# First layer's down-projection: sixth product ahead of the fifth, three norms set apart, two loads put under holds

## The chip, the cores and the metric

One core of a Trainium2 chip runs the whole program. The metric is the device time of one execution in microseconds (us). The reported time is the median of several runs.

## The reference, cut to what matters

The program is one inference step of a two-layer encoder on 1024 prompt rows and 8 x 16 sample rows, 1152 rows of 1024 columns, all float32. Each layer has a mixer and then a GEGLU channel mixer with a causal convolution, and each is closed by a layer norm. The part at hand is the end of layer 0's channel mixer: the down-projection and the norm behind it.

```python
ALPHA = (2 * DEPTH) ** 0.25                       # DEPTH = 2
...
out = (gelu(g) * a) @ w_down                      # (1152, 2816) @ (2816, 1024)
...
x = layer_norm(ALPHA * x + (1 + g_f) * f, ln_g[l, 1], ln_b[l, 1])
```

## The kernel before

The 1152 rows are nine tiles of 128. `down1` (L1466) multiplies the activations, 22 row blocks of 128 (`NFF`), kept transposed in DRAM as `actD`, by `wdn`. Tiles 0 to 5 go through a scheme of seven products in place of eight (Winograd's form of Strassen's): the inner dimension is paired, block 2m with 2m + 1 (`NK` = 11 steps), the rows are halved into tiles 0 to 2 and 3 to 5, and the columns into two halves of 512. Its operands are slices of `actD` and `wdn`, sums of them that earlier code has put in `actS` and `wT`, and for product 5 a difference of two halves of `wdn` that is made on the spot: two loads (L1536, L1537) and a subtraction on POOL (L1538).

A float32 product is three matmuls of rounded parts. For each operand SP loads it (L1498 weights, L1505 activations), ACT casts it to the high part (L184), and DVE subtracts to get the low part (L195). One step m of a product is nine matmuls (L1511): three tiles by three parts, 512 columns each, into three of the eight PSUM banks. With `keep` the last steps are gathered, so that each bank is finished, and read out by `done(i)`, before the next.

The order of the products before is 1 (banks A = 0, 1, 2), 2 (C = 5, 6, 7), 5 (B = 3, 4, 5), 6 (on top of 1 in A), 3 (on top of 5 in B), 7 (on top of 6 in A), 4 (B). The read-outs are `to_c11` (ACT copies C, DVE adds A: L1592, L1593), `to_p5`, `to_u2`, `to_c12` (L1603), `to_c22` (L1607, and ACT's copy L1608) and `to_c21`. `gate` multiplies by the gate (L1559), and `head` adds the residual (L1574), loaded by `fetch_row`.

`norm` calls `norm_tail`: statistics on DVE (L998 to L1002), a square root on ACT (L987) with its refinement on DVE (L988 to L992), a scaling on DVE (L1037), eight transposes on PE in two groups of four (L1047) into two banks, their read-out by DVE (L1055) and ACT (L1059, L1063), and writes to DRAM (L1066, L1068, L1072). Tiles 0 to 2 are normed while product 7 runs, at its steps 2, 5 and 8.

Tiles 8, 6 and 7 then go through a plain product, `block`, over 22 row blocks. Its weights come through `wload` (the load is L199), the first two in `ahead`, just before product 4's last steps. Tiles 3 to 5 are gated and normed inside its first steps.

The order of the instructions on each engine is set by a planner (a scheduler with a timeline model), which takes the code's order as a priority and moves instructions within their dependences. `with self.tc.issue_after(ins)` adds order edges from `ins` to instructions of the block. SP issues all loads and writes here, and at most eight are outstanding: each waits for the one eight before it.

Of the kernel before, what the change touches and what calls it, by code (L numbers as in the profile page):

```python
# [106 lines left out]
class Trunk:  # L107
# [1359 lines left out]
    def down1(self, xsrc, xdst, affs, act_sums):  # L1467
# [52 lines left out]
        def fetch(q, m):  # L1520
            e, o = 2 * m, 2 * m + 1
# [13 lines left out]
            r, b = diffs.next(), diffs.next()  # L1535
            nc.sync.dma_start(r, wdn[e][:, lo_half])  # L1536
            nc.sync.dma_start(b, wdn[e][:, hi_half])  # L1537
            nc.gpsimd.tensor_sub(r, b, r)  # L1538
            w = subs.next()
# [3 lines left out]
        def product(q, banks, new=True, keep=0, hook=None, ahead=lambda: None, done=lambda i: None):  # L1543
            for m in range(NK - keep):
                a, w = fetch(q, m)
                for i in range(3):
                    mm(self.bank(banks[i]), a, i, w, new and m == 0, m == NK - 1)
                if hook:
                    hook(m)
# [26 lines left out]

        A, B, C = (0, 1, 2), (3, 4, 5), (5, 6, 7)

# [23 lines left out]
        def to_c12(i):  # L1602
            nc.vector.tensor_add(u2[i], self.bank(B[i]), u2[i])  # L1603
            gate(u2[i], u2[i], i, 1)
# [6 lines left out]
        def to_c21(i):  # L1611
            nc.vector.tensor_sub(u3[i], u3[i], self.bank(B[i]))

        product(1, A, hook=start)
        aff = affs()
        product(2, C, keep=2, done=to_c11)
        product(5, B, done=to_p5)
        product(6, A, new=False, hook=norm_rows, done=to_u2)
        for t in range(3):
            fetch_row(t)  # L1620
        product(3, B, new=False, done=to_c12)

        hf1, rows = Ring([self.hf]), []

        def done(m):
            if m in (0, 3, 6):
                rows.append(head(m // 3))
            if m in (2, 5, 8):
                with self.tc.issue_after(self.downmm):
                    norm(m // 3, rows[m // 3], hf1, C[1:3])  # L1630

# [3 lines left out]
        def more(m):  # L1635
            if m in (1, 3, 6):
                fetch_row(3 + (1, 3, 6).index(m))

# [10 lines left out]
        def ahead():  # L1649
            nonlocal acts  # L1650
            self.ws, acts = Ring(plain), Ring(highs)
            firsts.extend(load(j) for j in range(2))

# [5 lines left out]
        keep = KEEP[0]  # L1659
        product(4, B, keep=keep, hook=more, ahead=ahead, done=to_c21)  # L1660
        rows = []
        for j in range(NFF - keep):
# [3 lines left out]
            if j == 0:  # L1666
                for i in range(3):
                    gate(u3[i], u3[i], 3 + i, 0)
                    rows.append(head(3 + i))
                self.take_w0(F32R)  # L1670
# [532 lines left out]
```

## Time and profile before

| what | us |
|---|---|
| median of 3 runs | 2722.82 |
| lowest, highest | 2721.62, 2728.88 |
| profiled execution | 2716.27 |
| its span | 2714.5 |
| PE busy | 2606.1 (96%) |
| DVE busy | 1980.8 (73%) |
| ACT busy | 1365.4 (50%) |
| POOL busy | 1028.1 (38%) |

PE is TensorE's matmuls, DVE VectorE, ACT ScalarE, POOL GpSimd, and SP the engine that issues transfers (SPq is its queue). A row of a timeline gives start, duration, engine, line, operation, output<-input and a count, and in brackets the engine's idle time ahead of it with what ended it. A stretch's PEclk is the granted clock of TensorE as a share of 2.4 GHz. "DMA share" is the mean busy share of the core's 16 DMA engines.

### The profile page before, as it was taken

What the parts mean: (1) busy time and instruction counts of PE and PEld (TensorE: products, weight loads), DVE (VectorE), ACT (ScalarE), POOL (GpSimd) and SP (SyncE); (2) the same over time, 40 slices, a digit from 0 to 9 for tenths busy, and PEclk for the clock granted to TensorE, in tenths of its full rate; (3) what the DMA queues carried; (4) which work ended last, traced back from release to release, by engine and by line L of the source; (5) the groups of instructions that cost most, each with busy time, mean ns of one, the idle gap of its engine ahead of it and who ended that gap; (6) DMA issues with size and microseconds to landing.
All of it is one profiled execution on the core that took longest, in us unless ns stands there. A gap on an engine that the chain in (4) does not pass through costs nothing.

```text
span 2714.5 us, 47659 instructions
## 1 busy us (share of the span) xinstructions
PE 2606.1 (96%) x17295; PEld 2326.4 (86%) x17295; DVE 1980.8 (73%) x3997; ACT 1365.4 (50%) x2855; POOL 1028.1 (38%) x792
## 2 busy tenths in 40 slices
PE   7999889999999999999999999989999999999997
PEld 6997768989999997878898888867899999998886
DVE  4476777787777687787854677777788877778668
ACT  3475734433343345654446666672445454556553
POOL 3032623367666644011220121252367666552101
PEclk9999999999999999999999999999999999999999
DMA  9656534566656548866758556783544334349673
GB/s 326 211 153 204 156 121 168 184 243 229 227 183 206 188 156 298 298 218 219 255 196 263 144 153 187 218 243 123 183 153 163 140 126 150 119 146 315 208 233 124
DMA packets 251564, 531.49 MB, mean 196 GB/s; under 512 B 39904, under 2 KB 108464, under 8 KB 251328
## 3 DMA queue, kind: packets, MB, share of 16 engines
q1 hardware_dynamic: 251328, 528.44, 59.3%
q8 instruction: 136, 2.23, 0.3%
q14 instruction: 100, 0.82, 0.1%
HBM read 396.17 MB, written 141.61 MB: 198 GB/s over the span
## 4 chain that ended last, share of the span: by engine, by line
PE 67%; DVE 12%; DMA 10%; ACT 4%; issue 4%; POOL 3%; SPq 1%; DVEq 0%; POOLq 0%; ACTq 0%
PE PS L1241 23%; PE PS L1511 9%; PE PS L327 8%; PE PS L314 8%; PE PS L1750 5%; PE PS L610 3%; PE PS L588 2%; DVE F L1290 2%; DVE wl L195 2%; PE PS L559 1%; PE PS L241 1%; PE PS L562 1%; PE PS L301 1%; DMA ws<-in_adaw_dram 1%; PE PS L737 1%
## 5 line engine op out<-in xcount | busy, mean ns | idle before, releaser
L1241 PE MATMUL PS<-H,wh 128*128 128x320 f32 (+1 forms) x2624 | 401.8, 294 | 0.0
L1241 PEld LDWEIGHTS PS<-H,wh 128*128 128x128 f32 x2624 | 364.5, 189 | 0.4 <-issue 0.4
L195 DVE TENSOR_TENSOR wl<-F,wh 128x512 fp32r<-128x512 f32 (+3 forms) x245 | 244.3, 1005 | 69.7 <-ACT wh L184 64.9
L1201 DVE TENSOR_TENSOR F<-PS,F 128x256 f32<-128x256 f32 (+1 forms) x446 | 196.1, 451 | 111.9 <-PE PS L1241 103.7
L184 ACT CAST wh<-F 128x512 fp32r<-128x512 f32 (+3 forms) x245 | 144.8, 602 | 248.0 <-PE PS L1241 125.9
L1241 PE MATMUL PS<-H,wl 128*128 128x256 f32 (+1 forms) x1312 | 230.5, 297 | 8.2 <-DVE wl L195 4.3
L1241 PEld LDWEIGHTS PS<-H,wl 128*128 128x128 f32 x1312 | 192.4, 189 | 17.0 <-issue 4.8
L1241 PE MATMUL PS<-xa,wh 128*128 128x320 f32 (+1 forms) x1328 | 204.3, 295 | 0.0
L1241 PEld LDWEIGHTS PS<-xa,wh 128*128 128x128 f32 x1328 | 185.7, 190 | 0.0
L648 POOL TENSOR_TENSOR F<-F,x2r 64x512 f32<-64x512 f32 x62 | 79.2, 1278 | 204.0 <-DVE F L624 170.6
L184 ACT CAST wh<-ws 128x512 fp32r<-128x512 f32 (+1 forms) x140 | 100.0, 717 | 110.3 <-DMA ws<-in_wup_dram 43.7
L1290 DVE SCALAR_TENSOR_TENSOR F<-F 128x1024 f32<-128x1024 f32 (+2 forms) x160 | 141.3, 929 | 7.9 <-ACT F L1329 7.5
L1361 POOL TENSOR_TENSOR F<-F 128x1152 f32<-128x1152 f32 x43 | 122.9, 2858 | 53.3 <-DVE F L1354 22.8
L184 ACT CAST H<-H 128x384 fp32r<-128x384 f32 (+3 forms) x158 | 94.4, 610 | 92.4 <-DMA H<-actD 52.8
L195 DVE TENSOR_TENSOR H<-H 128x384 fp32r<-128x384 f32 (+2 forms) x144 | 101.5, 720 | 51.6 <-ACT H L184 51.5
L195 DVE TENSOR_TENSOR wl<-ws,wh 128x512 fp32r<-128x512 f32 (+1 forms) x122 | 120.2, 987 | 25.8 <-ACT wh L184 21.7
L314 PE MATMUL PS<-H,w0r 128*128 128x384 f32 (+1 forms) x720 | 137.2, 340 | 0.3 <-ACT H L184 0.3
L327 PE MATMUL PS<-xa,H 128*128 128x512 f32 x504 | 128.4, 395 | 5.0 <-ACT xa L184 3.3
L526 DVE CUSTOM_DVE_ANT_0 F<-PS,F,C 128x256 f32<-128x256 f32 (+3 forms) x208 | 97.3, 480 | 49.2 <-PE PS L562 25.3
L314 PE MATMUL PS<-H,wh 128*128 128x384 f32 (+1 forms) x672 | 132.6, 339 | 0.0
L314 PEld LDWEIGHTS PS<-H,w0r 128*128 128x128 f32 x720 | 124.5, 188 | 2.3 <-ACT H L184 0.6
L1241 PE MATMUL PS<-xa,wl 128*128 128x256 f32 (+1 forms) x664 | 120.1, 302 | 4.6 <-DVE F L1201 2.8
(374 smaller groups left out, 6700.5 us busy)
## 6 DMA issues: line engine op xcount, KB each, us to landing
ws<-in_adaw_dram SPq DMA_DIRECT2D x63, 512.0 KB
ws<-in_wup_dram SPq DMA_DIRECT2D x51, 512.0 KB
F<-in_adaw_dram SPq DMA_DIRECT2D x49, 512.0 KB
w0f<-in_wdn_dram SPq DMA_DIRECT2D x44, 512.0 KB
F<-in_wup_dram SPq DMA_DIRECT2D x37, 512.0 KB
xa<-kH SPq DMA_DIRECT2D x60, 256.0 KB
F<-in_wdn_dram SPq DMA_DIRECT2D x60, 256.0 KB
xd<-F SPq DMA_DIRECT2D x27, 512.0 KB
```

Of the source, the lines that this page charges most:

```text
L184: nc.scalar.copy(out, in_)
L195: self.eng(el).tensor_sub(lo, src, hi.bitcast(F32))
L314: mm = self.nc.tensor.matmul(out[:, 0:n], w[a][:, k * 128 : k * 128 + 128], H[:, p, k, s0 : s0 + n], start=i == 0, stop=i == 23)
L327: self.nc.tensor.matmul(out[:, 0:n], H[:, p, j * kn + k, t0 : t0 + 128], w[a][:, k * n : k * n + n], start=i == 0, stop=i == 23,)
L526: nc.vector.tensor_tensor_reduce(out=p[:, c0 : c0 + w], in0=ps, in1=b, scale=1.0, scalar=init, op0=ALU.add, op1=ALU.min, accum_out=nm)
L610: mm = nc.tensor.matmul(ob[:, i0 * 128 : (i0 + n) * 128], vst[a][:, kt, :], pp[:, m * 128 : (m + n) * 128], start=cnt == 0, stop=cnt == to ...
L1201: nc.vector.tensor_add(d, v(ps), a if len(a.shape) == 3 else v(a))
L1241: self.pairmm = nc.tensor.matmul(ps[:, 0:m], w[a][:, k * 128 : k * 128 + 128], x(p, k, n), start=start and c == 0, stop=c == 11, skip_grou ...
L1290: nc.vector.scalar_tensor_tensor(o, u, cw[:, cc, i : i + 1], o, op0=ALU.mult, op1=ALU.add)
L1361: (nc.vector if l == 0 and j == NFF - 1 else nc.gpsimd).tensor_mul(yg, yg, ya)
L1511: self.downmm = nc.tensor.matmul(ps, a[p][:, i * 128 : i * 128 + 128], w[q], start=first and c == 0, stop=last and c == 2, skip_group_chec ...
L1750: self.downmm = nc.tensor.matmul(ps, a[p][:, i * 128 : i * 128 + 128], w[q], start=first and c == 0, stop=last and c == 2, skip_group_chec ...
```

## The change

Five things change in `down1`. Product 6 runs directly behind product 2, and product 5 after it with its last two steps gathered. Product 3 gets banks of its own (C = 6, 7, 5) instead of running on top of product 5, so that `to_c12` has one more addition for each of its three tiles; B is now (5, 3, 4) and product 4 has E = (3, 4, 5). The norm of tile 0 is called at step 6 of product 7, and those of tiles 1 and 2 at steps 1 and 5 of product 4. The gates of tiles 3 to 5 are spread over steps 0, 2 and 4 of the plain product, and residual loads come later. Two holds are written: the differences' loads and subtraction inside `issue_after` of a matmul six steps back, and the first plain loads inside one of two steps back.

```diff
@@ -1533,9 +1533,10 @@
                 return act(actS[m, 0][:, r2]), weight(wT[m, 0][:, hi_half])
             a = act(actS[m, 1][:, r2])
             r, b = diffs.next(), diffs.next()
-            nc.sync.dma_start(r, wdn[e][:, lo_half])
-            nc.sync.dma_start(b, wdn[e][:, hi_half])
-            nc.gpsimd.tensor_sub(r, b, r)
+            with self.tc.issue_after(steps[-6]):
+                nc.sync.dma_start(r, wdn[e][:, lo_half])
+                nc.sync.dma_start(b, wdn[e][:, hi_half])
+                nc.gpsimd.tensor_sub(r, b, r)
             w = subs.next()
             self.split(r, *w, "a", "v")
             return a, w
@@ -1545,6 +1546,7 @@
                 a, w = fetch(q, m)
                 for i in range(3):
                     mm(self.bank(banks[i]), a, i, w, new and m == 0, m == NK - 1)
+                steps.append(self.downmm)
                 if hook:
                     hook(m)
             kept = [(m, *fetch(q, m)) for m in range(NK - keep, NK)]
@@ -1574,7 +1576,8 @@
                 nc.vector.scalar_tensor_tensor(x[:, n], x[:, n], ALPHA, parts[hf], op0=ALU.mult, op1=ALU.add)
             return x
 
-        A, B, C = (0, 1, 2), (3, 4, 5), (5, 6, 7)
+        A, B, C, E = (0, 1, 2), (5, 3, 4), (6, 7, 5), (3, 4, 5)
+        steps = []
 
         def start(m):
             if m == 2:
@@ -1600,7 +1603,8 @@
             nc.scalar.copy(u2[i], self.bank(A[i]))
 
         def to_c12(i):
-            nc.vector.tensor_add(u2[i], self.bank(B[i]), u2[i])
+            nc.vector.tensor_add(u2[i], u2[i], p5[i])
+            nc.vector.tensor_add(u2[i], self.bank(C[i]), u2[i])
             gate(u2[i], u2[i], i, 1)
 
         def to_c22(i):
@@ -1609,32 +1613,36 @@
             gate(p5[i], p5[i], 3 + i, 1)
 
         def to_c21(i):
-            nc.vector.tensor_sub(u3[i], u3[i], self.bank(B[i]))
+            nc.vector.tensor_sub(u3[i], u3[i], self.bank(E[i]))
 
         product(1, A, hook=start)
         aff = affs()
         product(2, C, keep=2, done=to_c11)
-        product(5, B, done=to_p5)
-        product(6, A, new=False, hook=norm_rows, done=to_u2)
+        product(6, A, new=False, done=to_u2)
+        product(5, B, keep=2, done=to_p5)
         for t in range(3):
             fetch_row(t)
-        product(3, B, new=False, done=to_c12)
+        product(3, C, hook=norm_rows, done=to_c12)
 
         hf1, rows = Ring([self.hf]), []
 
         def done(m):
             if m in (0, 3, 6):
                 rows.append(head(m // 3))
-            if m in (2, 5, 8):
+            if m == 6:
                 with self.tc.issue_after(self.downmm):
-                    norm(m // 3, rows[m // 3], hf1, C[1:3])
+                    norm(0, rows[0], hf1, C[0:2])
 
         product(7, A, new=False, hook=done, done=to_c22)
         subs, acts = Ring(subs.items[4:12]), Ring(lows)
 
         def more(m):
-            if m in (1, 3, 6):
-                fetch_row(3 + (1, 3, 6).index(m))
+            if m in (1, 5):
+                with self.tc.issue_after(self.downmm):
+                    t = 1 + m // 5
+                    norm(t, rows[t], hf1, C[0:2])
+            if m in (3, 6):
+                fetch_row(2 + m // 3)
 
         slots = [tuple(X1[:, o + 1024 * a : o + 1024 * a + 1024] for a in range(2)) for o in (0, 3072, 5120, 7168)]
         self.wring = Ring([ws[1], ws[2], slots[0], ws[3], *slots[1:]])
@@ -1649,7 +1657,8 @@
         def ahead():
             nonlocal acts
             self.ws, acts = Ring(plain), Ring(highs)
-            firsts.extend(load(j) for j in range(2))
+            with self.tc.issue_after(steps[-2]):
+                firsts.extend(load(j) for j in range(2))
 
         def block(j, w, a, i, t):
             for hf in range(2):
@@ -1657,16 +1666,19 @@
                 mm(self.bank(GB[2 * i + hf]), a, t - 6, (w[0][:, n], w[1][:, n]), j == 0, j == NFF - 1)
 
         keep = KEEP[0]
-        product(4, B, keep=keep, hook=more, ahead=ahead, done=to_c21)
+        product(4, E, keep=keep, hook=more, ahead=ahead, done=to_c21)
         rows = []
         for j in range(NFF - keep):
             w, a = firsts[j] if j < 2 else load(j)
             for i, t in enumerate(GR):
                 block(j, w, a, i, t)
             if j == 0:
-                for i in range(3):
-                    gate(u3[i], u3[i], 3 + i, 0)
-                    rows.append(head(3 + i))
+                fetch_row(5)
+            if j in (0, 2, 4):
+                i = j // 2
+                gate(u3[i], u3[i], 3 + i, 0)
+                rows.append(head(3 + i))
+            if j == 4:
                 self.take_w0(F32R)
                 self.wring.items.append(ws[0])
             if j in (3, 7, 11):
```

How the orders move, at the places that the prediction speaks of.

SP, from the end of product 1's loads to those of the product after product 2. L983 loads the LN rows, L1498 a weight, L1505 activations, and L1536/L1537 (now L1537/L1538) the halves of a difference; the last row is product 2's last activation load. Before:

```order
L983 DMA F<-in_ln_dram 128x1024 x2
L1498 DMA ws<-in_wdn_dram 128x512
L1505 DMA H<-actS 128x384
L1537 DMA F<-in_wdn_dram 128x512
L1498 DMA ws<-in_wdn_dram 128x512 x2
L1505 DMA H<-actS 128x384
L1498 DMA F<-in_wdn_dram 128x512
L1536 DMA F<-in_wdn_dram 128x512
L1498 DMA F<-in_wdn_dram 128x512
L1505 DMA xa<-actD 128x384
```

and with the change:

```order
L1498 DMA ws<-in_wdn_dram 128x512 x3
L1498 DMA xa<-wT 128x512
L1505 DMA H<-actS 128x384
L1538 DMA F<-in_wdn_dram 128x512
L983 DMA F<-in_ln_dram 128x1024
L1505 DMA H<-actS 128x384
L1498 DMA xa<-wT 128x512
L983 DMA F<-in_ln_dram 128x1024
L1498 DMA F<-in_wdn_dram 128x512
L1505 DMA xa<-actD 128x384
```

The ranks up to here and the last row's are the same; weights of product 2 and 6 now stand ahead of the LN rows. The rows that follow directly, before:

```order
L1536 DMA F<-in_wdn_dram 128x512 x2
L1505 DMA H<-actS 128x384
L1378 DMA actS<-F 128x768
L1536 DMA F<-in_wdn_dram 128x512
L1378 DMA actS<-F 128x768
L1505 DMA H<-actS 128x384 x4
```

and with the change:

```order
L1498 DMA wl<-wT 128x512
L1498 DMA F<-in_wdn_dram 128x512
L1505 DMA H<-actS 128x384
L1498 DMA wl<-wT 128x512
L1378 DMA actS<-F 128x768
L1505 DMA H<-actS 128x384
```

The differences' loads have gone behind, and loads of `wT` for product 6 stand in their place.

ACT, from the cast of that activation (`xa<-xa 128x384`) to the copies of product 2's banks (L1592, now L1595). Before:

```order
L184 CAST xa<-xa 128x384
L184 CAST wh<-F 128x512
L184 CAST H<-H 128x384
L184 CAST wh<-F 128x512 x3
L184 CAST H<-H 128x384
L1592 COPY x2s<-PS 128x512
L184 CAST H<-H 128x384 x2
L1592 COPY x2s<-PS 128x512
L184 CAST H<-H 128x384
L1592 COPY x2s<-PS 128x512
```

and with the change:

```order
L184 CAST xa<-xa 128x384
L184 CAST wh<-wl 128x512
L184 CAST H<-H 128x384
L184 CAST wh<-wl 128x512
L184 CAST H<-H 128x384
L1595 COPY x2s<-PS 128x512
L184 CAST wh<-wl 128x512
L1595 COPY x2s<-PS 128x512
L184 CAST H<-H 128x384
L1595 COPY x2s<-PS 128x512
```

The casts of differences (`wh<-F`) are gone from here, and two casts each of product 6's weights and activations stand ahead of the first copy.

PE, from the last matmuls of product 7 to product 4's first steps and the plain product's first blocks. L1047 is a transpose. Before:

```order
L1511 MATMUL PS<-wh,H 128x512
L1047 MATMUL PS<-C,F 128x128 x12
L1511 MATMUL PS<-wh,H 128x512 x4
L1511 MATMUL PS<-wl,H 128x512
L1511 MATMUL PS<-wh,H 128x512 x2
L1511 MATMUL PS<-wl,H 128x512
L1511 MATMUL PS<-wh,H 128x512
L1511 MATMUL PS<-xa,H 128x512 x3
L1047 MATMUL PS<-C,F 128x128 x4
L1511 MATMUL PS<-wl,H 128x512
```

and with the change:

```order
L1511 MATMUL PS<-wh,H 128x512
L1047 MATMUL PS<-C,F 128x128 x8
L1511 MATMUL PS<-wh,H 128x512 x4
L1511 MATMUL PS<-wl,H 128x512
L1511 MATMUL PS<-wh,H 128x512 x2
L1511 MATMUL PS<-wl,H 128x512
L1511 MATMUL PS<-wh,H 128x512
L1511 MATMUL PS<-xa,H 128x512 x3
L1511 MATMUL PS<-wl,H 128x512
```

and somewhat further on with the change:

```order
L1511 MATMUL PS<-wl,H 128x512
L1511 MATMUL PS<-wh,H 128x512
L1047 MATMUL PS<-C,F 128x128 x8
L1511 MATMUL PS<-xa,H 128x512 x36
L1047 MATMUL PS<-C,F 128x128 x8
L1511 MATMUL PS<-xa,H 128x512 x12
```

Four transposes of tile 1 no longer stand directly behind tile 0's eight; tile 1's and tile 2's now follow as eights behind 27 and 36 more matmuls.

## Rows read from the trace of the kernel before

**Rows 1.** windows of 25 us: length; busy PE, PEld, DVE, ACT, POOL; PEclk; DMA share; GB/s

```profile
1050.00:1075.00 25.00, 18.81 (x81) 15.19 (x80) 11.76 (x16) 6.62 (x13) 14.30 (x10) 0.95 0.84 299
1075.00:1100.00 25.00, 25.00 (x102) 20.27 (x102) 18.90 (x27) 11.84 (x24) 7.62 (x6) 0.92 1.03 327
...
1125.00:1150.00 25.00, 25.00 (x112) 20.54 (x111) 15.37 (x26) 14.10 (x26) 0.00 (x0) 1.00 0.78 247
1150.00:1175.00 25.00, 19.98 (x92) 16.33 (x90) 23.39 (x54) 13.00 (x24) 0.00 (x0) 1.00 0.58 178
1175.00:1200.00 25.00, 23.77 (x101) 19.59 (x102) 19.53 (x30) 16.65 (x32) 8.56 (x3) 0.87 0.72 246
```

**Rows 2.** timeline of PE at the two stops

```profile
1074.10 7.25 PE L1511 MATMUL PS<-xa 128*128 128x512 f32 x20 [6.19 <-DVE xa L195]
...
1168.94 1.03 PE L1047 MATMUL PS<-C,F 128*128 128x128 f32 x8
1176.23 1.11 PE L1047 MATMUL PS<-C,F 128*128 128x128 f32 x4 [6.25 <-ACT F L1063]
1176.99 2.05 PE L1511 MATMUL PS<-wh,H 128*128 128x512 f32 x4
```

**Rows 3.** timeline of SP, the issues at and behind its two blocks

```profile
1043.67 0.33 SPq L1498 DMA_DIRECT2D w0f<-in_wdn_dram  x1
1052.95 0.33 SPq L1537 DMA_DIRECT2D F<-in_wdn_dram  x1
...
1058.04 2.01 SPq L983 DMA_DIRECT2D F<-in_ln_dram  x2
...
1067.70 0.33 SPq L1505 DMA_DIRECT2D xa<-actD  x1
...
1165.98 0.33 SPq L199 DMA_DIRECT2D ws<-in_wdn_dram  x1
...
1168.26 0.38 SPq L1498 DMA_DIRECT2D wl<-wT  x1
```

**Rows 4.** chain of waits through the stage: start, us, what

```profile
1067.70 5.21 DMA xa<-actD
...
1168.26 5.34 DMA wl<-wT
```

**Rows 5.** waits of SP's queue, 1040 to 1070 and 1150 to 1172: total, times, longest

```profile
SPq L1537 <- POOL F L1538: 8.6, 1, 8.6
...
SPq L199 <- DVE C L988: 9.1, 1, 9.1
```

**Rows 6.** timeline of POOL, the three subtractions

```profile
1043.74 11.70 POOL L1538 TENSOR_TENSOR F<-F 128x512 f32<-128x512 f32 x3 [4.10 <-DMA F<-in_wdn_dram]
```

**Rows 7.** small windows of PE: length, busy (matmuls), PEclk, DMA share, GB/s

```profile
1058.00:1060.00 2.00, 2.00 (x11) 1.00 0.81 224
...
1068.00:1072.00 4.00, 0.00 (x0) 1.00 1.06 385
...
1074.10:1080.00 5.90, 5.90 (x15) 0.56 1.06 394
...
1176.20:1182.00 5.80, 5.77 (x17) 0.53 0.59 216
```

**Rows 8.** timeline of ACT at the second stop

```profile
1173.03 0.51 ACT L184 CAST H<-H 128x384 fp32r<-128x384 f32 x1 [2.01 <-DMA H<-actD]
1173.68 0.62 ACT L184 CAST wh<-wl 128x512 fp32r<-128x512 f32 x1
1174.20 1.50 ACT L1059 ACTIVATE F<-PS,C 128x128 f32<-128x128 f32 x4
...
1176.94 0.62 ACT L1608 COPY x2s<-PS 128x512 f32<-128x512 f32 x1
```

**Rows 9.** timelines of ACT and DVE behind the first stop

```profile
1074.75 0.51 ACT L184 CAST H<-H 128x384 fp32r<-128x384 f32 x1 [0.78 <-DMA H<-actS]
...
1078.98 0.51 ACT L184 CAST H<-H 128x384 fp32r<-128x384 f32 x1
1079.39 0.58 ACT L1592 COPY x2s<-PS 128x512 f32<-128x512 f32 x1
...
1080.57 0.68 DVE L1593 TENSOR_TENSOR x2s<-PS,x2s 128x512 f32<-128x512 f32 x1
```

**Rows 10.** timeline of DVE, the scalings of tiles 3 to 5

```profile
1229.50 2.25 DVE L1037 TENSOR_SCALAR F<-F,C 128x1024 f32<-128x1024 f32 x3
```

## The prediction

> **What bounds the kernel now.** I read the stage's windows first, then the chain of waits, PE's timeline, the clock in small windows, and the timelines of SP, POOL, ACT and DVE at the places where PE stands. The stage runs from 1024 to 1297 us. In its windows PE is full, 25.00 of 25 us, except in two places, around 1070 and around 1172 [rows 1]. So nothing but these two stalls, and the slow clock after each, can give time back here: DVE, ACT, POOL and the transfers are hidden wherever PE reads 25.00.
>
> **Stall 1.** PE stops at 1067.91 and goes on at 1074.10, 6.19 us idle, released by DVE's split of xa [rows 2]. That xa is the last activation slice of product 2, from actD; SP issues its load only at 1067.70 [rows 3], and the chain runs through it, 5.21 us to its landing [rows 4]. It is late because SP is blocked from 1043.99 to 1052.95 at one load of a difference, whose buffer POOL is still reading [rows 3, 5], POOL's three subtractions there taking 11.70 us, 3.9 each [rows 6]. All later issues slide, and then run at full DMA share: 1.06, 385 GB/s [rows 7].
>
> **Stall 2.** PE does eight transposes at 1168.94 and stops until 1176.23, 6.25 us, because four transposes of the next tile stand at the head of its queue and need a bank that ACT empties last (L1063) [rows 2]. ACT's emptying, at 1174.20, stands behind casts whose loads landed at 1173.0 and 1173.6, the last from 1173.68 [rows 8]; the second, of 5.34 us, is in the chain [rows 4]; it was issued at 1168.26, after SP had stood 9.1 us at a plain weight load (L199) that waited for DVE's norm work [rows 3, 5].
>
> **The clock.** In both stalls the granted clock falls from 1.00 (2.4 GHz) to half (1.2 GHz) while PE stands, and comes back some 5 us after it runs again: the mean is 0.56 over 5.90 us of matmuls and 0.53 over 5.77 [rows 7]. Cost: 5.90 x 0.44 = 2.60 and 5.77 x 0.47 = 2.71 us. The stage thus holds 6.19 + 2.60 + 6.25 + 2.71 = 17.75 us in all.
>
> **The change, part by part**, against the profiled execution: span 2714.5, 2716.27 with the 1.77 us around it, 6.55 below the median shown (2722.82). I add the sum to the median.
>
> *The two holds cost and give nothing.* issue_after binds only instructions of its block on the engine of the instruction named, and that is PE; the held blocks hold SP, POOL, ACT and DVE work only. With the two holds taken out of the changed kernel, the order on all five engines is the same row for row. So the difference loads that jam SP at 1043.67 to 1052.95 are issued at the same rank, and so is the plain weight at 1165.98.
>
> *Stall 1.* SP's order is the same up to the two LN-row loads (512 KB each) at 1058.04 [rows 3]. From there to the late xa the change puts three weight loads first and draws the LN rows later; the bytes ahead of the late load are the same 3,200 KB, which at 385 GB/s [rows 7] set its landing. The two LN rows cost SP 2.01 us where transfers were not saturated, 224 GB/s [rows 3, 7]; moved behind, up to (1 - 224/385) x 2.01 = 0.8 us comes back, of which I count half or a little more. I take -0.5, bounds -2.0 to +2.0 (the three weight loads' 768 KB at 385 GB/s, either way).
>
> *Product 6 in place of product 5 at that point.* Before, product 5 followed in banks 3, 4 and 5, of which 3 and 4 were free. Now product 6 accumulates on banks 0 to 2, which DVE must first read (L1593, now L1596), behind ACT's copy. Its first matmul comes nine matmuls after 1074.10. Fifteen took 5.90 us there at a mean clock of 0.56 [rows 7], so one takes 0.393 x 0.56 / 0.50 = 0.44 us at half clock, and PE is ready at 1074.10 + 9 x 0.44 = 1078.1. The copy now stands on ACT behind two weight casts and two activation casts. Before, the first activation cast behind the late xa came at 1074.75 and the second only at 1078.98, with the copy at 1079.39 and the add from 1080.57 to 1081.25 [rows 9]. Now the last cast ahead of the copy needs a transfer with 1,536 KB behind the late xa instead of 1,920 KB, so about 384 KB / 385 GB/s = 1.0 us sooner than before, and POOL's differences no longer stand in between: copy near 1077.5, add done near 1078.8. Wait 0.7; bounds 0 and 3.2 (as late as before, 1081.25 - 1078.1).
>
> *Product 6's transfers*: 192 + 256 KB a step of nine matmuls against 192 + 512 for product 5. Before, the heavier one ran at 327 GB/s with PE at 25.00 [rows 1], and the lighter is hidden too: 0. Product 5 comes after it with a product's time for its differences: 0.
>
> *Three more DVE additions*, 3 x 0.68 = 2.04 us [rows 9]. They fall where DVE is busy 15.37 of 25 us [rows 1]: hidden, 0; uncovered they would cost 2.04.
>
> *Norms set apart.* SP's order up to the jam, and DVE's up to the evictions of tile 0, are unchanged, with the statistics and the scaling of all three tiles still together; so the first weight load of product 4 is still issued at 1168.26 [rows 3]. What moves is PE's queue: tile 1's transposes leave the head, and product 4's first three matmuls stand there. They need the activation's split and ACT's weight cast at 1173.68, done by 1174.35 [rows 8]. So they start then instead of at 1176.99 [rows 2], 4.4 us after PE's stop, run 3 x 0.44 = 1.3 us, and PE stands again until the copy of bank 2 (L1608, from 1176.94, [rows 8]) is done at 1177.5; before, that next matmul ran at 1176.99 + 1.3 = 1178.3. Gain 0.8. Bounds: 0 (the copy later by that much) and 0.8 + 2.71 = 3.5, if this shorter stop leaves the clock at 2.4 GHz. I take 0.8, since 4.4 us is nearer to stall 1's 6.19, which lost the clock, than to none.
>
> *Later*: the transposes of tiles 3 to 5 are drawn forward by 25 matmuls, 5.6 us at 112 in 25 us [rows 1], and their scaling on DVE (three in 2.25 us, [rows 10]) by about as much; one scaling late is 0.75: 0 to +1, I take +0.2. Rows of layer 1's output projection change places by one or two: one more scaling or one less ahead of a transpose, -0.75 to +0.75, taken 0.
>
> Sum: -0.5 + 0.7 - 0.8 + 0.2 = -0.4. **2722.82 - 0.4 = 2722.4 us: no change.** A measurement here tells no change from 0.3% (8.2 us).
>
> **Rivals.**
> 1. *One stall goes* (most likely the first): if the reordered issues break the queue ahead of xa, 6.19 + 2.60 = 8.8 come back: 2714.0. For: the wait is at one transfer only. Against: the same jam, the same bytes [rows 5]. 0.13.
> 2. *Both go*, which is what the two holds would mean if they acted: 17.75, so 2705.1. Against: the orders. 0.06.
> 3. *The clock stays up in stall 2*: -3.5 + 0.4 from the rest, 2719.7, still within 0.3%. 0.12.
> 4. *Slower: product 6 stands at its banks.* It decides when DVE's first addition out of bank 0 ends: later than 1078.1 PE waits. At before's time it costs 3.2, and since PE then stands again at half clock, its return may start anew, another 5.90 x 0.44 = 2.6: 3.2 + 2.6 - 0.5 - 0.8 = +4.5, with the late norms' +1 some 2728.3. For: the copies stand behind casts of the very loads that are late. Against: fewer bytes ahead of them. 0.13. The Trainium skill, Perfetto Trace Analysis (Optimizing Tensor Performance, Matmuls), says that matmul groups should rotate through PSUM banks so that the emptying of one overlaps the next group's work; product 6 on the banks of product 1 goes against that. No row of before shows such a wait, since product 5 stood between; by the page the 3.2 would be the rule rather than the bound.
>
> **How the numbers follow.** Forecast 0.56 (2720.5 to 2726), the rivals 0.13, 0.06, 0.12 and 0.13. Faster by over 0.3% takes rivals 1 and 2 and a little unforeseen: 0.21. Slower by over 0.3% needs rival 4 at its worst and more: 0.09. The same: 0.70. The range, 2710 to 2730, leaves out rival 2, part of rival 1 and the far end of rival 4; the three runs of before alone lie 7.3 us apart.
>
> **What would show it.** SP still blocked some 9 us near 1044, released by POOL; PE idle 5 to 7 us near 1068, released by DVE's xa; at product 6's start a short wait at DVE's L1596; near 1170 PE idle twice, 4.4 and 2 us, with eight transposes instead of twelve in a row. The steps are wrong if the difference load is no longer blocked, if the xa load leaves before 1065, or if PE waits over 2 us at L1596.

## The result and the profile after

The changed kernel takes 2727.77 us (median of 22 runs, 2719.98 to 2736.14), the kernel before, run beside it, 2722.9 (22 runs, 2717.67 to 2730.77). The ratio is 1.0018, 95% interval 1.0010 to 1.0026: 4.9 us slower (2.7 to 7.1). I had forecast no change, 2722.4 us. The time lies in my range and under the 0.3% that I called no change, but the change has a sign, and it is not the one of my sum (-0.4). The profiled execution takes 2727.01 us, with a span of 2725.2.

An execution's span (first to last instruction) says little here. The order of PE and SP is the same in both kernels up to the stage, and yet the stage began anywhere from 1024.01 us (before) to 1035.58 in the executions profiled. So I compare two stretches that I can cut out of any trace. The **stage** runs from the first matmul of the split products (L1511) to the first of the next projection (L327). The **late stretch** runs from the first matmul of layer 1's output projection (the second block of L327) to the first of L1241. The whole stage as one window of PE (length, busy, granted clock, DMA share, GB/s), of the kernel before:

```profile
1024.01:1296.62 272.61, 260.17 (x1139) 0.97 0.76 256
```

and of the kernel after:

```profile
1030.53:1305.12 274.59, 261.58 (x1139) 0.97 0.75 254
```

The stage is 1.98 us longer: PE stands 0.57 us more (13.01 against 12.44), and its busy time is 1.41 us longer for the same matmuls, which goes with the clock: the half clock cost 8.6 us here against 6.8 (table further on). PE's timeline at its stops in the kernel after (start, us, engine, line, operation, count, idle before and releaser) answers to [rows 2]:

```profile
1080.76 4.21 PE L1511 MATMUL PS<-xa 128*128 128x512 f32 x9 [6.65 <-DVE xa L195]
1085.44 1.43 PE L1511 MATMUL PS<-xa 128*128 128x512 f32 x5 [0.48 <-DVE x2s L1596]
...
1134.43 1.89 PE L1511 MATMUL PS<-xa,H 128*128 128x512 f32 x7 [0.90 <-ACT w0f L1600]
...
1177.29 1.03 PE L1047 MATMUL PS<-C,F 128*128 128x128 f32 x8
1182.42 1.62 PE L1511 MATMUL PS<-wh,H 128*128 128x512 f32 x3 [4.10 <-DVE H L195]
1184.91 0.79 PE L1511 MATMUL PS<-wh,H 128*128 128x512 f32 x1 [0.88 <-ACT x2s L1612]
```

Four of these I had named: the stop on xa, the short wait of product 6 at its bank (L1596), and the second stop in two parts, 4.10 and 0.88. The one at 1134.43 I had not. It is the turn from product 5 to product 3: product 3's third bank is bank 5, with which product 5 began, and its copy (L1600) comes late.

The chain behind the first stop is unchanged, as [rows 3, 5] had it: SP is blocked at a difference's load by POOL, and xa leaves late. (What POOL does in that time I had misread from [rows 6]; see the last section.) SP's timeline at its block, and the late xa at its end:

```profile
1049.49 0.50 SPq L1498 DMA_DIRECT2D w0f<-in_wdn_dram  x1
1059.42 0.33 SPq L1538 DMA_DIRECT2D F<-in_wdn_dram  x1
...
1073.32 0.38 SPq L1505 DMA_DIRECT2D xa<-actD  x1
```

SP's waits there (line, releaser, total, times, longest; the second line is its wait ahead of the second stop):

```profile
SPq L1538 <- POOL F L1539: 9.1, 2, 8.6
SPq L199 <- DVE C L988: 8.8, 1, 8.8
```

The clock answers to [rows 7]. Windows of PE behind the first stop, and behind the second:

```profile
1080.76:1086.00 5.24, 4.76 (x11) 0.57 1.05 402
1086.00:1088.00 2.00, 2.00 (x10) 1.00 1.06 381
...
1182.42:1190.00 7.58, 6.70 (x15) 0.50 0.54 199
1190.00:1192.00 2.00, 2.00 (x7) 0.72 0.00 0
```

Behind the first stop the clock is back as soon as before. Behind the second, in two parts now, PE ran at half clock beyond 1190 in this execution, some 2.5 us of running longer than before (0.53 over 1176.2 to 1182 in [rows 7]).

### The profile page after: what moved, and what is told of

It reads as the page before. It is cut to its first block, busy times and chain, and to the rows that moved or that the text cites. A ratio compares the mean times of both kernels' runs of the same rounds, so it can differ in the third digit from the quotient of the medians.

```text
span 2725.2 us, 47671 instructions
## 1 busy us (share of the span) xinstructions
PE 2617.5 (96%) x17295; PEld 2334.5 (86%) x17295; DVE 1990.6 (73%) x4000; ACT 1367.5 (50%) x2855; POOL 1033.3 (38%) x792
## 4 chain that ended last, share of the span: by engine, by line
PE 73%; DVE 10%; DMA 8%; ACT 3%; issue 3%; POOL 3%; SPq 1%; DVEq 0%; POOLq 0%; ACTq 0%
PE PS L1241 28%; PE PS L327 11%; PE PS L314 8%; PE PS L1511 8%; PE PS L1762 5%; PE PS L610 3%; PE PS L588 2%; PE PS L241 2%; DVE wl L195 1%; DVE F L1290 1%; PE PS L559 1%; PE PS L301 1%; PE PS L562 1%; DVE xa L195 1%; PE PS L737 1%
## 5 line engine op out<-in xcount | busy, mean ns | idle before, releaser
L1241 PE MATMUL PS<-H,wh 128*128 128x320 f32 (+1 forms) x2624 | 403.1, 295 | 0.0
L1241 PEld LDWEIGHTS PS<-H,wh 128*128 128x128 f32 x2624 | 365.7, 189 | 0.4 <-issue 0.4
L1241 PE MATMUL PS<-H,wl 128*128 128x256 f32 (+1 forms) x1312 | 230.4, 297 | 8.2 <-ACT F L1208 4.8
L1241 PEld LDWEIGHTS PS<-H,wl 128*128 128x128 f32 x1312 | 192.6, 189 | 16.4 <-ACT F L1208 5.5
L1241 PE MATMUL PS<-xa,wh 128*128 128x320 f32 (+1 forms) x1328 | 203.4, 294 | 0.0
L1241 PEld LDWEIGHTS PS<-xa,wh 128*128 128x128 f32 x1328 | 184.6, 189 | 0.0
L195 DVE TENSOR_TENSOR H<-H 128x384 fp32r<-128x384 f32 (+2 forms) x144 | 95.3, 675 | 59.7 <-ACT H L184 59.4
L327 PE MATMUL PS<-xa,H 128*128 128x512 f32 x504 | 131.7, 403 | 4.9 <-ACT xa L184 3.3
L1241 PE MATMUL PS<-xa,wl 128*128 128x256 f32 (+1 forms) x664 | 119.8, 301 | 4.0 <-DVE F L1201 2.4
```

The source lines that it names most:

```text
L195: self.eng(el).tensor_sub(lo, src, hi.bitcast(F32))
L327: self.nc.tensor.matmul(out[:, 0:n], H[:, p, j * kn + k, t0 : t0 + 128], w[a][:, k * n : k * n + n], start=i == 0, stop=i == 23,)
L1241: self.pairmm = nc.tensor.matmul(ps[:, 0:m], w[a][:, k * 128 : k * 128 + 128], x(p, k, n), start=start and c == 0, stop=c == 11, skip_grou ...
```

## Experiments

Each kernel was timed in five rounds against the kernel before. The theory that I went in with: the new product order brings two new waits in the stage, setting the norms apart is worth nothing there, and the late stretch, whose instructions the planner puts into another order, costs the rest. Its rivals: all of it is the product order, or all of it the norms.

**e_order: the products alone.** The kernel before with the new product order, banks and three extra additions; the norms stay together.

```diff
-        A, B, C = (0, 1, 2), (3, 4, 5), (5, 6, 7)
+        A, B, C, E = (0, 1, 2), (5, 3, 4), (6, 7, 5), (3, 4, 5)
...
-        product(5, B, done=to_p5)
-        product(6, A, new=False, hook=norm_rows, done=to_u2)
+        product(6, A, new=False, done=to_u2)
+        product(5, B, keep=2, done=to_p5)
...
-        product(3, B, new=False, done=to_c12)
+        product(3, C, hook=norm_rows, done=to_c12)
```

> The kernel before with the new order of products alone (6 ahead of 5, product 3 in banks of its own); norms, gates and residual loads as before. The order of layer 1 stays as before up to three matmuls. Theory A (the new order brings two waits into the stage): in the profile PE stands near 1070 for 6 to 7 us as before, then some 0.5 us at L1596 and 0.9 us at the copy of product 5's first bank; +1.5 to +2.5 us against before. Theory B (the whole loss of the change is in the new order): +4 to +6. Theory C (it is all in the norms): -0.5 to +0.5.

Measured: 2722.2 us against 2723.63, ratio 0.9996 (0.9983 to 1.0009); stage 272.69. PE's timeline at the bank of product 6:

```profile
1079.19 3.70 PE L1511 MATMUL PS<-xa 128*128 128x512 f32 x9 [5.55 <-DVE xa L195]
1084.02 1.65 PE L1511 MATMUL PS<-xa 128*128 128x512 f32 x6 [1.12 <-DVE x2s L1595]
```

Both new waits are there (1.12 us at the bank, 1.62 at the turn to product 3), the first stop is shorter by as much as executions differ, and the late stretch keeps before's order (172.92 us). The 1.5 to 2.5 us that I expected didn't show in the total, whose interval runs from -4.6 to +2.5 us: the products alone don't bring the whole of the loss, and a small loss can't be told from none.

**e_norms: the norms alone.** The kernel before with the norms of tiles 1 and 2 moved into product 4 and the gates and heads spread.

```diff
-            if m in (2, 5, 8):
+            if m == 6:
...
-            if m in (1, 3, 6):
-                fetch_row(3 + (1, 3, 6).index(m))
+            if m in (1, 5):
+                with self.tc.issue_after(self.downmm):
+                    t = 1 + m // 5
+                    norm(t, rows[t], hf1, C[1:3])
```

> The kernel before with the norms of tiles 1 and 2 moved into product 4, and the gates, heads and residual loads of tiles 3 to 5 spread, as in the change; products in the old order. Theory A: near 1170 PE stands twice, some 4 and 1 us, in place of 6.25, but the half clock lasts 8 to 9 us in place of 5.8, so that the stage gains nothing (-0.5 to +0.5), and the reordered output projection of layer 1 costs 1 to 2.5: +1 to +2.5 in all. Theory B: 0. Theory C: +4 to +6.

Measured: 2721.6 us, ratio 0.9998 (0.9982 to 1.0014); stage 271.24. PE at the second stop:

```profile
1182.83 1.15 PE L1511 MATMUL PS<-wh,H 128*128 128x512 f32 x3 [3.91 <-DVE H L195]
1185.82 0.80 PE L1511 MATMUL PS<-wh,H 128*128 128x512 f32 x1 [1.85 <-ACT x2s L1608]
```

That is the split I had forecast, 4.4 and 1.9 us: 5.76 in all against 6.25 [rows 2]. The half clock behind it lasted 6.8 us (1183.4 to 1190.2), as in the kernel before, and not the 8 to 9 that I expected. The total shows no loss either (interval -4.9 to +3.8 us, expected +1 to +2.5).

**x_after_dif: a hold that holds.** The changed kernel, with the differences' loads tied to an earlier load on SP in place of an instruction of PE.

```diff
-            nc.sync.dma_start(raw, src)
+            wloads.append(nc.sync.dma_start(raw, src).ins)
...
-            with self.tc.issue_after(steps[-6]):
+            with self.tc.issue_after(wloads[-6]):
```

> The changed kernel with the differences' hold made to act: their loads are queued on SP behind the weight load of six steps earlier, in place of behind a matmul. Theory A (SP blocked at a difference makes the late activation load): SP is no longer blocked 9 us near 1044, product 2's last activation load leaves 7 us or more earlier, PE's stop of 6 us near 1070 and its half clock go, and the time falls by 7 to 10 us against the change, some 2718 to 2720. Rival (the queue is full anyway, or product 6's or 5's own loads are late next): a stop of the same size at another load, within 2 us of the change.

Measured: 2717.93 us, ratio 0.9984 (0.9969 to 1.0000); stage 268.20. SP's timeline where it stood blocked before:

```profile
1047.07 0.33 SPq L1500 DMA_DIRECT2D w0f<-in_wdn_dram  x1
...
1054.56 1.03 SPq L983 DMA_DIRECT2D F<-in_ln_dram  x2
...
1056.31 0.33 SPq L1507 DMA_DIRECT2D xa<-actD  x1
```

No difference stands there any more, xa leaves 17 us sooner than in the changed kernel, and the 6-us stop is gone. What is left there is 0.46 us at the bank and 2.16 at a weight cast; the stop at the turn to product 3 is gone as well. By the two ratios this is some 9 us under the changed kernel, as expected (7 to 10). The first stop was SP's block at the difference, and the change's own hold doesn't touch it.

**e_nohold: the change without its two holds.**

```diff
-            with self.tc.issue_after(steps[-6]):
...
-            with self.tc.issue_after(steps[-2]):
```

> The changed kernel without its two holds (the differences' loads and the first plain loads are issued with no edge to a product step). Theory (holds bind nothing on SP, since the edge leads to a PE instruction that POOL's or SP's own order has behind it anyway): the order of every engine is the changed kernel's, so the time is the changed kernel's too: 2724 to 2731 us, ratio to before 1.000 to 1.003, and the trace has the same four stops of PE in the stage (about 6.6 us on xa, 0.5 on x2s, 0.9 on L1600's copy or its counterpart, 4 on H), stage length 274 +-2 us. Rival (the holds delay loads and are what made the change slower): 2719 to 2723 us, ratio below 1.000, and fewer or shorter stops.

Measured: 2726.92 us against 2720.96, ratio 1.0028 (1.0013 to 1.0043); stage 275.70, with the same stops (4.84, 1.01, 2.32, 4.04, 0.84 us). The holds do nothing: PE, POOL and SP run the stage in the same order without them, and this is the changed program a second time. Where its third stop is 2.32 us long, the clock falls there as well.

**y_bef_rot: the second stop's cause.** The kernel before, with the rings of product 4's buffers turned by two, so that its first loads don't ask for buffers that product 7's last steps still read. In SP's order of before, the loads of product 4's steps 2 to 7 stand ahead of the plain load at L199, and those of steps 0 and 1 behind it; with the turn it is steps 0 to 5 ahead, and 6 and 7 behind. SP's wait at L199 stays.

```diff
-        subs, acts = Ring(subs.items[4:12]), Ring(lows)
+        subs, acts = Ring(subs.items[6:12] + subs.items[4:6]), Ring(lows[2:] + lows[:2])
```

> The kernel before with product 4's rings of weight and activation buffers started two slots further on, at buffers that product 3 and not product 7 read last. Theory A (what makes the stop near 1170 is that product 4's first loads wait for buffers which product 7's last two steps still read, and not SP's block at the plain weight): its first loads leave 8 us or more earlier, the stop of 6.25 us and the half clock behind it go, -6 to -9 us. Rival (the plain weight load's block, or ACT's emptying of the transposes, sets it): the stop stays above 4 us and the time within 2 us of before.

Measured: 2720.95 us, ratio 0.9983 (0.9967 to 0.9999); stage 265.94; no stop behind the eight transposes, which come at 1177.78 here, and 0.54 and 0.95 us later on. SP's wait there and PE's timeline:

```profile
SPq L199 <- DVE C L988: 8.2, 1, 8.2
```

```profile
1177.78 1.04 PE L1047 MATMUL PS<-C,F 128*128 128x128 f32 x8
1178.57 6.38 PE L1511 MATMUL PS<-xa,H 128*128 128x512 f32 x27
```

By its ratio the kernel is 4.6 us faster than before, less than the 6 to 9 expected; part of that may be the late order, which is the changed kernel's here (table below). SP still stands 8.2 us at the plain load, and PE no longer cares: product 4 had been given, for the steps it runs first, the buffers that come free last.

**y_best: both.** The changed kernel with the real hold and the turned rings (the two diffs above).

> The changed kernel with the hold of the differences tied to an earlier load on SP (so SP is really held to the order) and with the rings of product 4's buffers turned by two, so that its first loads don't ask for the buffers that product 7's last steps read. Theory: the stop of 6.6 us and the one of 4.1 us both go, with the time at half clock behind them; stage length 258 to 264 us instead of 274.6; the late order is that of the changed kernel (not of before), so of the 10 to 16 us some 1 to 3 are given back; 2710 to 2717 us, ratio 0.995 to 0.998. Rival 1 (product 4's loads then queue elsewhere, another stop takes the second's place): stage 266 to 270, 2717 to 2721 us. Rival 2 (late order costs as much as the stage gains): stage about 260 and yet 2719 to 2723 us.

Measured: 2716.96 us against 2720.96, ratio 0.9982 (0.9968 to 0.9995); stage 260.76. One window over the stage:

```profile
1028.08:1288.84 260.76, 256.18 (x1139) 1.00 0.79 268
```

The clock never falls in this stage (1.00). What PE still stands is 4.58 us in pieces of under 1.6. The stage is 11.85 us shorter than in the profile of before; the total gains 4.0 by the medians and 4.9 by the ratio (1.4 to 8.7), at the low edge of what I expected. Less came through than the stage gained.

**x_order_dif: the real hold under the new products, with the old norms** (e_order with this):

```diff
+            wloads.append(nc.sync.dma_start(raw, src).ins)
...
+            with self.tc.issue_after(wloads[-6]):
```

> The kernel before with the new order of the products, and the differences' loads held behind an earlier load on SP; norms as before, late order as before. Theory (the first stop is SP's wait on POOL, and goes with the real hold whatever the norms do): stage 266 to 269 us against 272.7 without the hold, no stop on xa, the stop of about 4.5 us on F stays; 2716 to 2720 us, ratio 0.997 to 0.9990. Rival (the first stop only moves to the next load in SP's order): stage 271 to 273, 2721 to 2724 us.

Measured: 2719.56 us, ratio 0.9989 (0.9974 to 1.0004); stage 266.80; no stop on xa (1.40 us remain at the bank, 1.65 at a weight cast), the second stop stays (5.86 us on F). The first stop goes by the hold whatever the norms do; the total moved less than its noise.

**p_after, q_before, p_best, after_again: the late order by itself.** In the late stretch, 110 places of PE's order, 39 of DVE's, 14 of ACT's and 2 of SP's differ between the two kernels, though the change edits no line there. Order edges along those rows (in_rows: each instruction behind the one that stands ahead of it in the other kernel) put one kernel's order into the other:

```diff
         program(tc, I, O)
+        in_rows(tc)
```

p_after is the changed kernel with before's late order, q_before the reverse (but for one SP load two places earlier), p_best is y_best with before's late order, and after_again is the changed kernel beside them.

> The changed kernel with the rows of PE, DVE, ACT and SP in layer 1's output projection put back into the order that the kernel before has there, by order edges along those rows; all else is the changed kernel's. Theory (the change costs 2 to 3 us in the stage and the rest in the output projection's other order): output projection 173 to 173.5 us instead of 174 to 176.6, no stop of 1.25 us or more in it; total 1 to 3 us below the changed kernel of this call, 2723 to 2726 us, ratio to before 1.0000 to 1.0015. Rival (the order there is worth nothing, all of the difference is the stage or the spread of executions): within 1 us of the changed kernel of this call, ratio 1.0018 to 1.003.

> The kernel before with the rows of PE, DVE, ACT and SP in layer 1's output projection put into the changed kernel's order. Theory: the first product stage as before (272 to 273 us, its stops of 6.2 and 6.25 us); output projection 174 to 176.6 us with a stop of 1.25 to 1.7 us on ACT's F; 1 to 3 us above before, ratio 1.0003 to 1.0012. Rival: ratio 0.9990 to 1.0003, output projection 173.2.

> The kernel with the real hold and the turned rings (stage 260.8 us) with the output projection's rows in the order of before. Theory: stage 259 to 262 us, output projection 173 to 173.5; 2711 to 2716 us, ratio 0.9955 to 0.998. Rival (what the stage gains is given back elsewhere, not in that order): 2716 to 2719 us, ratio 0.998 to 0.999 as with the changed kernel's order.

> The changed kernel once more, beside the three others on one chip. Theory: ratio to before 1.001 to 1.003, stage 274 to 276 us, output projection 173.5 to 176.6. Rival (its excess was a chip's or an hour's): ratio 0.9990 to 1.0005.

Measured, all beside 2722.62 us of before: p_after 2722.92, ratio 1.0002 (0.9987 to 1.0017); q_before 2724.39, 1.0007 (0.9997 to 1.0017); p_best 2714.24, 0.9975 (0.9962 to 0.9987); after_again 2726.72, 1.0017 (1.0006 to 1.0028). All profiled executions, sorted by their late order, with PE's idle time and what the half clock cost (the sum of (1 - granted clock) x length over windows of 2 us, so with its share of the stops):

| kernel | stage | PE idle in it | clock | late stretch |
|---|---|---|---|---|
| before | 272.61 | 12.44 | 6.8 | 173.20 |
| e_order | 272.69 | 12.80 | 5.1 | 172.92 |
| x_order_dif | 266.80 | 8.91 | 3.4 | 173.37 |
| p_after | 273.95 | 14.13 | 6.8 | 173.67 |
| p_best | 259.98 | 4.29 | 0 | 173.04 |
| e_norms, a third order | 271.24 | 11.16 | 6.8 | 172.36 |
| x_after_dif, that order | 268.20 | 8.52 | 5.1 | 173.86 |
| after | 274.59 | 13.01 | 8.6 | 173.90 |
| after_again | 275.12 | 13.20 | 8.5 | 174.14 |
| e_nohold | 275.70 | 13.05 | 8.5 | 176.57 |
| c_copy (below) | 273.48 | 11.73 | 8.5 | 174.54 |
| q_before | 269.29 | 10.46 | 5.1 | 175.18 |
| y_bef_rot | 265.94 | 7.80 | 3.4 | 174.59 |
| y_best | 260.76 | 4.58 | 0 | 174.55 |

q_before's stage is shorter than I expected (269.29 us, not 272 to 273), with stops of 5.10 and 5.36: so far apart are two executions of a stage with the same order.

The seven executions with the changed kernel's late order (after and all below it) take longer there than the seven others, the nearest two by 0.04 only: 174.78 on the mean against 173.20, 1.6 us. In all seven PE stands for 0.38 to 1.69 us (1.2 on the mean) at a bank that ACT empties (L1303), in none of the others. PE's timeline there, in the changed kernel:

```profile
1989.82 2.45 PE L314 MATMUL PS<-H,wh 128*128 128x388 f32 x13
1993.52 1.68 PE L314 MATMUL PS<-H,wl 128*128 128x388 f32 x8 [1.25 <-ACT F L1303]
```

and with before's late order put in (p_after):

```profile
1990.10 1.57 PE L314 MATMUL PS<-H,wl 128*128 128x388 f32 x8
1991.50 2.97 PE L314 MATMUL PS<-H,wh 128*128 128x388 f32 x16
1994.31 1.57 PE L314 MATMUL PS<-H,wl 128*128 128x388 f32 x8
```

The stretch as I cut it ends too early to hold all of the cost. Some 8 us behind its end PE waits for ACT again, at the copy of another bank (L1208), in before and in after:

```profile
2008.30 0.85 PE L1241 MATMUL PS<-H,wl 128*128 128x320 f32 x4 [1.20 <-ACT F L1208]
```

```profile
2019.13 0.86 PE L1241 MATMUL PS<-H,wl 128*128 128x320 f32 x4 [2.21 <-ACT F L1208]
```

This wait is 1.92 to 2.50 us in the seven executions and 0.76 to 1.99 in the others, though PE's order is the same there in all. From the start of the late stretch to the first matmul of layer 1's split products the seven take 622.85 to 626.00 us (before 622.54, after 623.50) and the others 620.86 to 622.77: 2.3 us on the mean, with p_after 2.9 under the mean of after, after_again and e_nohold, p_best 3.2 under y_best and q_before 2.3 over before.

The timings point the same way in all three pairs (by the ratios p_after 4 us under after_again, and 2 us each p_best under y_best, which was timed on another chip, and q_before over before), each within its own noise. p_best beats both kernels.

**c_copy: the unforeseen stop.** One instruction of the changed kernel moved: on ACT the copy L1600 of product 5's first bank five rows earlier, ahead of the casts of product 3's loads, by order edges along the rows of ACT, DVE and SP there.

> The changed kernel with one instruction moved: on ACT the copy of product 5's first bank (L1600) five rows earlier, ahead of the casts of product 3's loads behind which it stood; every other row of every engine is the changed kernel's. Theory (the third stop of 0.9 to 2.0 us at the turn from product 5 to product 3 is this copy's place in ACT's queue: PE is done with the bank some 4 us before the copy starts): the stop there is gone or under 0.4 us and the clock stays up there, the other stops stay; stage 272 to 274 us instead of 274.6 to 275.7; total 1 to 3 us below the changed kernel, 2724 to 2726 us, ratio to before 1.0000 to 1.0015. Rival (PE would wait for the late loads of product 3 at the next step anyway): a stop of the same 0.9 to 2 us within 5 us behind the turn, on xa, H or wh; stage 274.6 to 275.7, ratio 1.0015 to 1.003.

Measured: 2727.81 us against 2724.05, ratio 1.0012 (0.9995 to 1.0028); stage 273.48. ACT's timeline in the changed kernel:

```profile
1132.98 0.51 ACT L184 CAST H<-H 128x384 fp32r<-128x384 f32 x1
1133.39 0.51 ACT L184 CAST xa<-xa 128x384 fp32r<-128x384 f32 x1
1133.81 0.57 ACT L1600 COPY w0f<-PS 128x512 f32<-128x512 f32 x1
```

and in c_copy ACT's, then PE's:

```profile
1132.03 0.58 ACT L1600 COPY w0f<-PS 128x512 f32<-128x512 f32 x1
1132.51 0.62 ACT L184 CAST wh<-ws 128x512 fp32r<-128x512 f32 x1
```

```profile
1133.61 8.32 PE L1511 MATMUL PS<-xa,H 128*128 128x512 f32 x36
```

PE runs through the turn, and nothing takes the stop's place: it was that copy's rank on ACT. The four executions in which the differences are really held on SP (x_after_dif, x_order_dif, y_best, p_best) have no stop at this turn either. The median didn't follow (expected 2724 to 2726). In the profiled execution the clock stayed at half longer behind the first stop, and PE's idle time fell by 1.6 us (13.35, the mean of the four, to 11.73) while its busy time did not; 1.6 us is below what twelve runs resolve.

## Why the prediction was wrong, point by point

The changed kernel's stage was profiled four times (after, after_again, e_nohold, p_after: mean 274.84 us), before's twice (before, q_before: 270.95): +3.9, of which idle time is +1.9 (13.35 against 11.45) and busy time +2.0 (261.49 against 259.50); before's two differ by 3.3 from each other. With the 2.3 us of the late order that makes 6.2, against 4.9, 4.6 and 7.6 measured for this program by the ratios of after, after_again and e_nohold. What the timings can say of the two shares favours the late one: p_after keeps the changed stage (273.95), and its total is before's (ratio 1.0002, -3.5 to +4.6 us).

- *The two holds cost and give nothing*: right. e_nohold has the same stops and the same time, and x_after_dif shows what a hold on SP's own queue does.
- *Stall 1*, -0.5 forecast: that SP's block makes it was right (x_after_dif), the 3.9 us each for POOL's three subtractions were not: one takes 9 to 10 us, the two others 1.3 each (last section). The change in its size is not to be told. It measured 6.65, 5.37, 4.84 and 6.96 us against 6.19 and 5.10: +0.3 on means, with a spread of 2 us within one program.
- *Product 6 at its banks*, +0.7 forecast: 0.48, 0.63, 1.01 and 0.85, mean 0.74. Right. The Trainium skill asks for a rotation of banks (Perfetto Trace Analysis, Optimizing Tensor Performance, Matmuls); the trace agrees that leaving it brings a wait, of this size and not of the 3.2 of my upper bound.
- *Norms set apart*, -0.8 forecast: 4.98, 5.03, 4.88 and 5.90 in two parts against 6.25 and 5.36: -0.6. Right in size and form. But its cause as I told it, SP's 9.1 us at the plain load, was half of it: y_bef_rot keeps that wait (8.2) and has no stop. The wait hurt only because product 4's steps 0 and 1 were loaded into the buffers that come free last, and so behind it.
- *Product 6's transfers ... Product 5 comes after it ...: 0*. **Here is the first step that failed.** I priced the moved products by their transfers and by the one bank turn ahead of product 6, and not the turn behind product 5, where product 3 now needs product 5's first bank and ACT's copy stands behind casts of late loads. It cost 0.90, 2.02, 2.32 and 0.42 us, mean 1.4. c_copy shows that the stop is that copy's place; its total, 1.0012 (0.9995 to 1.0028), doesn't resolve what the stop is worth.
- *The clock.* I let each stop cost what it cost before, and only allowed a gain. **That is the second step that failed**: the half clock cost 8.6, 8.5, 8.5 and 6.8 us in the four changed stages against 6.8 and 5.1 in before's, and busy time rose by 2.0. The third stop, where it came to 2 us (after_again, e_nohold), brought the clock down anew. Behind the second stop, cut in two, the clock stayed at half for 10.2 us in after and e_nohold but for 6.8 in after_again, p_after and e_norms, as in before (6.8; 3.4 in q_before): that a cut stop by itself holds the clock down longer is not shown.
- *Later ... Rows of layer 1's output projection change places: taken 0*, bounds -0.75 to +0.75. **The third step that failed**, in size, and the one that the timings bear out best: +1.6 in the stretch and +2.3 with what follows it, because the changed order there brings a stop at a bank further on (L1303) and lengthens the next (L1208), which counting scalings did not show. p_after, q_before and p_best show that it is the order.
- *Transposes of tiles 3 to 5*, +0.2 forecast: nothing. The five stops listed from the kernel after make up the whole of its 13.01 us.
- *Three more DVE additions*: no stop names them, and e_order, which has them, is not measurably slower. Hidden, as forecast.

So the forecast's terms held about where they had a place in the trace of before, and what I had put at nothing was three small things of one sign. Rival 4 came out near the time (2728.3) but not by its mechanism, the wait at product 6's banks. Rivals 1, 2 and 3 did not happen, and x_after_dif, y_bef_rot and y_best show what they would have taken: one real hold and a turn of two rings.

What stays open: how much of the stage's 3.9 us is in the measured total. Neither half of the change alone costs time that shows (e_order 272.69, e_norms 271.24 in the stage), neither has the changed kernel's late order, and two or three microseconds in the stage are within what one profiled execution differs from another. Why the planner turns the late order with this change, and with y_bef_rot, but with neither half of it alone, was not traced. And p_best shortens the stage by 11 us against the mean of before, while the median falls by 8.4 (interval of the ratio: 3.5 to 10.3 us).

## What to carry to other kernels

When products change places, price every bank turn that is new, not only the first: for each, look up where the copy that frees the bank stands in its engine's queue, and what that queue is waiting for. Ask of an order edge on which engine it acts: tied to a matmul the hold changed nothing (e_nohold), tied to a load on SP's own queue it held the loads (x_after_dif). And where a planner sets the order, compare the orders to the end of the program and follow a moved row to the next banks that are emptied: here a third of the loss or more lay 700 us behind the edit. And part a merged row before dividing it by its count.

## What I had not expected of the hardware

The program ahead of the stage is the same in all kernels, and its time is not. The granted clock differs in a stretch where PE is busy 86 of 100 us. The same window of PE, 300 to 400 us, in the kernel before:

```profile
300.00:400.00 100.00, 85.97 (x608) 0.97 0.43 132
```

and in the kernel after:

```profile
300.00:400.00 100.00, 86.53 (x590) 0.90 0.40 126
```

By this the stage began 1024.01 us in, or 1030.53; a spread that one execution can't be corrected for, except by cutting the stretch out as above.

POOL's subtractions of 128x512 differ by a factor of over seven. [rows 6] shows three as one row of 11.70 us, and I read them as 3.9 each. Parted, POOL's timeline in the kernel after is:

```profile
1049.56 9.84 POOL L1539 TENSOR_TENSOR F<-F 128x512 f32<-128x512 f32 x1 [3.46 <-DMA F<-in_wdn_dram]
1059.36 2.54 POOL L1539 TENSOR_TENSOR F<-F 128x512 f32<-128x512 f32 x2
1063.81 1.30 POOL L1539 TENSOR_TENSOR F<-F 128x512 f32<-128x512 f32 x1 [1.91 <-DMA F<-in_wdn_dram]
```

and DVE's, where a run without gaps ends:

```profile
1057.68 0.55 DVE L195 TENSOR_TENSOR H<-H 128x384 fp32r<-128x384 f32 x1
1065.43 0.56 DVE L195 TENSOR_TENSOR H<-H 128x384 fp32r<-128x384 f32 x1 [7.20 <-ACT H L184]
```

So one subtraction takes 9.84 us (9.18 in before) and the ten others 1.29 to 1.93. In all ten executions without the real hold there is one such, of 8.91 to 9.84 us, and it ends 1.15 to 1.17 us behind the last instruction of DVE's run. In the four with the hold none takes more than 2.18, and there is no stop on xa. SP's block, and with it the first stop, is this one instruction: it ends at 1059.40, and SP issues the load at 1059.42. A busy DVE is not the whole reason, since most of the later ones, of 1.29 to 1.93 us, ran beside a DVE just as busy; no run moved DVE's work away, so what holds POOL there is not shown.
